# Three of eleven pairs of down-projection tiles as seven block products, in an encoder trunk on one core

## The chip, the cores and the metric

The kernel runs on one core of a Trainium2 chip. A core has the engines PE (TensorE: matmuls and transposes), DVE (VectorE), ACT (ScalarE), POOL (GpSimd) and SP (SyncE, here only a DMA queue). Each engine takes its own instructions in the order of its queue and waits on semaphores for the others. The metric is the device time of one execution in microseconds (us); less is better.

## The reference

Four layers, post-norm. The mixer is chunked band attention in layers 0 and 3, a gated linear attention in layer 1, differential attention in layer 2. Behind each mixer stands a dense SwiGLU feed-forward. All is float32; 256 tokens, width 1024, hidden width 2816.

```python
def swiglu(x, w_gate_up, w_down):
    g, u = jnp.split(x @ w_gate_up, 2, axis=-1)
    return (jax.nn.silu(g) * u) @ w_down

for i in range(DEPTH):                      # DEPTH = 4
    y = mixer_i(h)
    h = layer_norm(DN_ALPHA * h + y, ln1_g[i], ln1_b[i])
    h = layer_norm(DN_ALPHA * h + swiglu(h, ffn_w_gate_up[i], ffn_w_down[i]), ln2_g[i], ln2_b[i])
```

## The kernel before

A float32 product is made from two reduced-precision halves of each operand (type fp32r): a high part, which is a cast, and a low part, which is the difference of the value and its cast. A block product of two 128-row operands is three matmuls: high by high, low by high, high by low. Two functions issue them. `run_rows` has the tokens as the stationary side and 512 output columns, so one product is three matmuls of 128x512 (L176 to L178). `run_cols` has 128 weight columns as the stationary side and the 256 tokens as the moving one; there a product is one matmul of 512 columns (both parts of the tokens) and one of 256 (L197, L198).

**Weights.** `w_tiles` takes two k-tiles (256 rows) by 512 columns at a time: SP issues one load of 512 KB into a ring of 6 raw tiles (L110), ACT casts 128x1024 to the high part (L111), DVE subtracts to get the low part (L112), into rings of 8 tiles each.

**Activations.** `split_T` transposes 128x128 blocks on PE (L225) and `put` splits the result: a cast on ACT (L212), a subtraction on DVE (L213).

**Order.** The program is written in one order and a scheduler sets each engine's queue from it. Work that belongs behind a product (transposes, gates, norms) is put off with `defer` by a count of products (the D_ numbers); `tick` counts them.

**Feed-forward.** `ffn` (L844) computes hidden blocks of 256 columns. The first two blocks go through `run_rows` and `row_done` (silu on ACT at L856, product on DVE at L858, then `split_T`); the other nine go through `run_cols` and `col_done` (copy L869, additions L870, silu L872). All hidden values are kept as high and low parts, in 22 k-tiles. The down projection is one call of `run_rows`: 2 column halves x 22 k-tiles x 2 token blocks = 88 products, 264 matmuls in a layer.

**Norm.** `Norm.part` adds the residual (L277) and takes statistics (L288) as each half of the columns comes; `finish` aggregates (L301), has POOL compute the reciprocal root (`rstd_of`, L246 and L250), and scales (L308, L320). `late_load` brings gains and biases: POOL copies one column of a tile that stands for the right time (L123) and then issues the load (L124).

**Gated linear attention.** `gla` (L608) first sets up constants on POOL: a tile `cst` with a triangle of ones and the norm's gain (memset L614, L617 to L619, load L628), `g1t` for the first gate's weights (memset L638), `g2` for the second gate's weights and bias (memset L647, loads L648 to L650). Then `gate1` (L668), `gate2` (L688) and `gate3` (L701, L706) follow one another for each block of 128 tokens, among the products of the stage. The constants come from a pool of tiles (`k2`) that all stages share, eight deep.

**Start.** 16 transposes of the identity (L905) into an otherwise idle bank.

Of the kernel before, what the change touches and what calls it, by code (L numbers as in the profile page):

```python
# [25 lines left out]
RAWB = 6  # L26
WB = 8
WARM = 16
# [4 lines left out]
D_NORM, D_HIDDEN = 8, 4  # L33
# [3 lines left out]
def trunk_kernel(  # L37
# [30 lines left out]
    wp = ctx.enter_context(tc.tile_pool(name="wp", bufs=1))  # L68
    act = ctx.enter_context(tc.tile_pool(name="act", bufs=1))
# [7 lines left out]

    def slab(shape, dtype=F32):
        return act.tile(shape, dtype, tag="slab", bufs=4, name=nm("slab"))

    def k3(shape, dtype=F32):
        return act.tile(shape, dtype, tag="k3", bufs=5, name=nm("k3"))

    def k2(shape, dtype=F32):
        return act.tile(shape, dtype, tag="k2", bufs=8, name=nm("k2"))

    def k1(shape, dtype=F32):
        return act.tile(shape, dtype, tag="k1", bufs=6, name=nm("k1"))
# [13 lines left out]
    def w_tiles(chunk, s, fine=False):  # L102


        raw = wp.tile([P, 2, 512], F32, tag="raw", bufs=RAWB, name=nm("raw"))
        wh = wp.tile([P, 2, 512], F32R, tag="wh", bufs=WB, name=nm("wh"))
        wl = wp.tile([P, 2, 512], F32R, tag="wl", bufs=WB, name=nm("wl"))
# [10 lines left out]
        return [(wh[:, k, :], wl[:, k, :]) for k in range(2)]  # L118

# [22 lines left out]
    def run_rows(chunks, lag=LAG, order=None, fine=0):  # L142
# [16 lines left out]
        for t, c, kt in order:  # L159
# [9 lines left out]
            b = banks[c, t]  # L169
            first = count[c, t] == 0  # L170
# [67 lines left out]

    def kt_of(op):
        return lambda kt: op[:, kt, :]  # L240
# [14 lines left out]
    class Norm:  # L255
        def __init__(self, h, g_ap, b_ap, out_ap=None):
# [4 lines left out]
            self.g = act.tile([P, D], F32, tag="lng", bufs=1, name=nm("lng"))  # L261
            self.b = act.tile([P, D], F32, tag="lnb", bufs=1, name=nm("lnb"))
            self.loads = [
                (self.g, g_ap.partition_broadcast(P)),
                (self.b, b_ap.partition_broadcast(P)),
            ]

        def load(self, seen):

            if self.loads:  # L270
                late_load(*self.loads.pop(0), seen)

        def part(self, n):
            def done(t, y):
                z = self.h[t]
                cs = slice(n * 512, (n + 1) * 512)
                nc.vector.scalar_tensor_tensor(  # L277
                    out=z[:, cs],
                    in0=z[:, cs],
                    scalar=ALPHA,  # L280
                    in1=y,
                    op0=ALU.mult,
# [15 lines left out]
        def finish(self, t, st):  # L298
# [5 lines left out]
            if not last and self.xT is None:  # L304
                self.xT = operand()
# [712 lines left out]
```

## Time and profile before

| What | Value |
|---|---|
| Runs | 1207.79, 1210.9, 1211.17 us; median 1210.9 us |
| Profiled execution | 1210.89 us, of which the profiled span is 1209.2 us |
| PE busy | 1192.0 us, 99% of the span |
| DVE busy | 828.9 us, 69% |
| ACT busy | 664.4 us, 55% |
| POOL busy | 97.9 us, 8% |
| Chain of work that ended last | PE 94%, DVE 2% |

Busy time of PE is the time in which a matmul is under way; matmuls are pipelined, so the spacing of their starts is shorter than the length shown for one. In a group or a timeline row `out<-in` are the program's names for the tiles, and the line number is that of the kernel before. The granted clock of PE is 0.99 or more of full speed in nearly all of the span.

### The profile page before, as it was taken

To read this page: it belongs to the slowest core of one execution; us is meant where nothing else is said; L and a number is where in the kernel's file an instruction comes from. 1 tells how busy PE (TensorE), PEld (TensorE's weight loads), DVE (VectorE), ACT (ScalarE), POOL (GpSimd) and SP (SyncE) were. 2 spreads that over 40 slices of the span, in tenths; PEclk is the share of its full clock that TensorE was granted. 3 is DMA by queue.
4 is the path that set the end of the run, shared out by engine and by line. 5 is a ranking of instruction groups with operands and counts; after the bars stand their busy time and mean duration, and the time that the engine had idled before them with its cause. 6 is when DMAs were issued, how large, how long until landed. Compare 5 with 4: busy or idle time off the path is not lost.

```text
span 1209.2 us, 17119 instructions
## 1 busy us (share of the span) xinstructions
PE 1192.0 (99%) x6240; PEld 994.6 (82%) x6240; DVE 828.9 (69%) x1418; ACT 664.4 (55%) x1169; POOL 97.9 (8%) x188
## 2 busy tenths in 40 slices
PE   7999999999999999999999999999999999999997
PEld 6888888888787888888887778888888888888885
DVE  6688866755656766774757787667476988676644
ACT  6566565644664355663446656656345775565531
POOL 1130000000001100000012110000011200000000
PEclk9999999999999999999999999999999999999999
DMA  9654656556474456555664355665566644655641
GB/s 358 207 191 139 207 179 224 193 175 192 140 244 122 152 182 241 197 183 184 191 222 149 118 169 188 219 209 187 176 193 220 191 138 151 204 205 184 206 142 35
DMA packets 62772, 223.88 MB, mean 185 GB/s; under 512 B 7264, under 2 KB 7776, under 8 KB 62688
## 3 DMA queue, kind: packets, MB, share of 16 engines
q1 hardware_dynamic: 57600, 206.60, 51.9%
q0 software_dynamic: 4512, 15.14, 3.5%
q10 hardware_dynamic: 576, 1.05, 0.3%
q8 instruction: 49, 0.80, 0.3%
q14 instruction: 35, 0.29, 0.1%
HBM read 221.71 MB, written 1.05 MB: 184 GB/s over the span
## 4 chain that ended last, share of the span: by engine, by line
PE 94%; DVE 2%; ACT 1%; DMA 1%; POOL 1%; issue 0%; POOLq 0%; DVEq 0%; ACTq 0%
PE mm L197 28%; PE mm L176 15%; PE mm L177 15%; PE mm L178 15%; PE mm L198 15%; PE tp L225 2%; PE tp L423 2%; ACT k L446 1%; PE tp L492 1%; DVE k L431 1%; DMA k<-in_c_bias_dram 1%; PE tp L513 0%; PE tp L515 0%; PE tp L514 0%; PE tp L755 0%
## 5 line engine op out<-in xcount | busy, mean ns | idle before, releaser
L112 DVE TENSOR_TENSOR wl<-raw,wh 128x1024 fp32r<-128x1024 f32 (+1 forms) x394 | 476.1, 1213 | 173.8 <-ACT wh L111 170.3
L197 PE MATMUL mm<-slab,wh 128*128 128x512 f32 x1568 | 553.8, 396 | 0.0
L111 ACT CAST wh<-raw 128x1024 fp32r<-128x1024 f32 (+1 forms) x394 | 407.1, 1047 | 199.6 <-PE mm L177 186.7
L198 PE MATMUL mm<-slab,wl 128*128 128x256 f32 x1568 | 441.0, 281 | 0.0
L197 PEld LDWEIGHTS mm<-slab,wh 128*128 128x128 f32 x1568 | 294.1, 188 | 69.7 <-issue 4.6
L176 PE MATMUL mm<-wh,slab 128*128 128x512 f32 x784 | 309.9, 396 | 6.1 <-ACT wh L111 6.1
L177 PE MATMUL mm<-wh,slab 128*128 128x512 f32 x784 | 307.4, 392 | 0.0
L178 PE MATMUL mm<-wl,slab 128*128 128x512 f32 x784 | 306.5, 391 | 0.0
L198 PEld LDWEIGHTS mm<-slab,wl 128*128 128x128 f32 x1568 | 296.5, 189 | 0.7 <-issue 0.3
L176 PEld LDWEIGHTS mm<-wh,slab 128*128 128x128 f32 x784 | 147.3, 188 | 38.8 <-ACT wh L111 6.1
L177 PEld LDWEIGHTS mm<-wh,slab 128*128 128x128 f32 x784 | 147.5, 188 | 31.1 <-issue 1.5
L178 PEld LDWEIGHTS mm<-wl,slab 128*128 128x128 f32 x784 | 147.3, 188 | 30.4 <-DVE wl L112 0.3
L870 DVE TENSOR_TENSOR k<-mm,k 128x256 f32<-128x256 f32 x144 | 60.5, 420 | 79.4 <-ACT k L869 79.4
L869 ACT COPY k<-mm 128x256 f32<-128x256 f32 x144 | 53.6, 372 | 67.4 <-PE mm L198 67.1
L872 ACT ACTIVATE k<-k 128x256 f32<-128x256 f32 x72 | 29.8, 414 | 46.7 <-DVE k L870 46.7
L246 POOL TENSOR_SCALAR sm<-mv 128x1 f32<-128x1 f32 x16 | 14.0, 874 | 499.3 <-DVE mv L301 499.3
L212 ACT CAST slab<-k 128x256 fp32r<-128x256 f32 (+1 forms) x76 | 31.8, 418 | 38.8 <-DVE k L876 37.5
L213 DVE TENSOR_TENSOR slab<-k,slab 128x256 fp32r<-128x256 f32 (+1 forms) x76 | 33.0, 434 | 22.8 <-ACT slab L212 22.8
L446 ACT ACTIVATE k<-k,nmx 128x128 f32<-128x128 f32 x96 | 42.5, 444 | 8.4 <-DVE nmx L442 8.3
L212 ACT CAST slab<-tp 128x512 fp32r<-128x512 f32 (+1 forms) x56 | 27.1, 495 | 31.9 <-PE tp L225 29.3
L213 DVE TENSOR_TENSOR slab<-tp,slab 128x512 fp32r<-128x512 f32 (+1 forms) x56 | 30.6, 569 | 8.6 <-ACT slab L212 8.6
L431 DVE CUSTOM_DVE_ANT_0 k<-tp,k 128x128 f32<-128x128 f32 x96 | 28.5, 352 | 10.2 <-PE tp L423 9.0
(135 smaller groups left out, 675.5 us busy)
## 6 DMA issues: line engine op xcount, KB each, us to landing
raw<-in_w_gu_dram SPq DMA_DIRECT2D x176, 512.0 KB, 4.4
raw<-in_w_down_dram SPq DMA_DIRECT2D x88, 512.0 KB, 4.2
raw<-in_a_qkv_dram SPq DMA_DIRECT2D x46, 512.0 KB, 4.7
raw<-in_b_in_dram SPq DMA_DIRECT2D x24, 512.0 KB, 3.6
raw<-in_c_qkv_dram SPq DMA_DIRECT2D x24, 512.0 KB, 3.7
raw<-in_a_o_dram SPq DMA_DIRECT2D x16, 512.0 KB, 4.1
k<-in_a_bias_dram POOLq DMA_DIRECT2D x16, 256.0 KB, 4.4
lng<-in_ln_g_dram POOLq DMA_DIRECT2D x8, 512.0 KB, 5.6
```

Of the source, the lines that this page charges most:

```text
L111: nc.scalar.copy(out=wh[:, k, :], in_=raw[:, k, :])
L112: nc.vector.tensor_tensor(out=wl[:, k, :], in0=raw[:, k, :], in1=wh[:, k, :].bitcast(F32), op=ALU.subtract,)
L176: nc.tensor.matmul(b, xh, wh, start=first, stop=False)
L177: nc.tensor.matmul(b, xl, wh, start=False, stop=False)
L178: nc.tensor.matmul(b, xh, wl, start=False, stop=last)
L197: nc.tensor.matmul(b, wh[:, cs], xk, start=kt == 0, stop=False)
L198: nc.tensor.matmul(b[:, :256], wl[:, cs], xk[:, :256], start=False, stop=kt == NKT - 1)
L212: nc.scalar.copy(out=h, in_=val)
L213: nc.vector.tensor_tensor(out=dst[:, ks, slice(256 + cs.start, 256 + cs.stop)], in0=val, in1=h.bitcast(F32), op=ALU.subtract,)
L446: nc.scalar.activation(pr[:, m, SL[t]], pr[:, m, SL[t]], AF.Exp, bias=nmx[:, t, m : m + 1], accum_out=sm[:, t, m : m + 1],)
L869: nc.scalar.copy(out=lo, in_=b[:, 256:])
L870: nc.vector.tensor_tensor(out=lo, in0=b[:, :256], in1=lo, op=ALU.add)
```

## The change

**Down projection.** The weights are laid out by pairs of k-tiles: `w_down[layer, c]` is 128x2048, the four blocks (two k-tiles by two halves of 512 columns) of pair c, loaded in 1 MB pieces. For pairs 0, 3 and 6 of the 11 (`SEVEN`) the 2x2 product of blocks (two token blocks by two k-tiles, times two k-tiles by two column halves) is made from seven block products where it was eight, by the Winograd form: the blocks of hidden values are combined with four additions (`combine`, on POOL), the blocks of weights with four (three DVE instructions, `load`), the seven products go into banks that `FORMS` and `where` name, and `gather` adds them into the residual at the last such pair. The other eight pairs keep eight products. The last three pairs finish token block 0 first, then block 1. A product's three matmuls come in another order (high by low first).

**Memory.** The weight rings are counted in bytes (24 KB raw, 64 KB split, as deep as before for ordinary pairs). `k2`, `k3` and `slab` come from a pool that is opened for each stage (`in_stage`) and reuses the memory of the stage before tile by tile. The next stage's input has a tile of its own (`xT`). Gains and biases of a norm are loaded as four 128x512 tiles.

**Start.** 24 transposes, written into the first bank that the products use.

```diff
-D_NORM, D_HIDDEN = 8, 4
+D_NORM, D_HIDDEN, D_COMBO = 8, 4, 5
+WARM = 24
+SEVEN = (0, 3, 6)
...
+    def in_stage(fn, *args, **kw):
+        with tc.tile_pool(name=nm("stage"), bufs=1, reuse_waits="tile") as pool:
...
     def k2(shape, dtype=F32):
-        return act.tile(shape, dtype, tag="k2", bufs=8, name=nm("k2"))
+        return st(shape, dtype, "k2", 12)
...
+    def halves(w, n):
+        wh = split_ring.tile([P, n, 512], F32R, name=nm("wh"))
+        wl = split_ring.tile([P, n, 512], F32R, name=nm("wl"))
+        nc.scalar.copy(out=wh, in_=w)
+        nc.vector.tensor_tensor(out=wl, in0=w, in1=wh.bitcast(F32), op=ALU.subtract)
...
+            for _ in range(warm):
+                nc.tensor.transpose(b[:, :P], ident, ident)
+            warm = 0
...
+        def combine(c):
+            f = hidden.pop(c)
+            a11, a12, a22, s1, s2, s3, s4, a21 = (f[:, i, :] for i in range(8))
+            nc.gpsimd.tensor_tensor(out=s1, in0=a21, in1=a22, op=ALU.add)
+            nc.gpsimd.tensor_tensor(out=s2, in0=s1, in1=a11, op=ALU.subtract)
+            nc.gpsimd.tensor_tensor(out=s3, in0=a11, in1=a21, op=ALU.subtract)
+            nc.gpsimd.tensor_tensor(out=s4, in0=a12, in1=s2, op=ALU.subtract)
+            defer(D_COMBO, lambda: split(c, f))
+
+        def split(c, f):
+            x = seven[c] = st([P, 2, 7, P], F32R, "seven", len(SEVEN))
+            nc.scalar.copy(out=x[:, 0], in_=f[:, 0:7, :])
+            nc.vector.tensor_tensor(
+                out=x[:, 1], in0=f[:, 0:7, :], in1=x[:, 0].bitcast(F32), op=ALU.subtract
+            )
...
-                defer(D_HIDDEN, lambda: split_T(hd, hid[0], t, 2 * c, 2))
+                defer(D_HIDDEN, lambda: turn_hidden(c, t, hd))
...
+            h11 = halves(raw[:, 0:1], 1)
+            diff(tt[:, 0:2, :], raw[:, 1:3, :], raw[:, 0:2, :])
+            diff(t2, tt[:, 1, :], b11, ALU.add)
+            ht = halves(tt, 3)
+            diff(t4, b21, t2)
+            parts[c] = h11 + halves(raw[:, 1:4], 3) + ht
...
+            nc.tensor.matmul(o, xh, wl, start=start, stop=False)
+            nc.tensor.matmul(o, xh, wh, start=False, stop=False)
+            nc.tensor.matmul(o, xl, wh, start=False, stop=stop)
...
+        FORMS = {
+            1: (0, 0), 6: (4, 6), 5: (3, 4), 7: (5, 5), 2: (1, 3), 3: (6, 2), 4: (2, 1),
+        }
...
+        tail = range(n_pairs - 3, n_pairs)
+        load(0)
+        for c in range(n_pairs - 3):
+            load(c + 1)
+            if c in SEVEN:
+                seven_products(c)
+                continue
...
-    idle = bank()
-    for _ in range(WARM):
-        nc.tensor.transpose(idle[:, :P], ident, ident)
```

On ACT, in layer 0 where the feed-forward goes from row products to column products, the queue before (casts of weights wh, silu of the last row block L856, casts of transposed hidden values into the operand):

```order
L212 CAST slab_1381<-tp_1498 128x2x128 [waits PE_49]
L111 CAST wh_1654<-raw_1653 128x1024 [waits DVE_49,DMAHW4_49,PE_49,Activation_49]
L111 CAST wh_1660<-raw_1659 128x1024 [waits DVE_49,DMAHW5_49,PE_49,Activation_49]
L856 ACTIVATE k_338_1518<-mm_1488 128x256 [waits PE_49,Activation_49]
L212 CAST slab_1381<-tp_1559 128x2x128 [waits PE_49]
```

and after (hid: the hidden blocks of a seven pair; seven: their operand with the sums; L932 is the silu):

```order
L959 COPY hid_1441<-tp_1518 128x128 [waits PE_49]
L960 COPY hid_1441<-tp_1518 128x128
L130 CAST wh_1679<-raw_1678 128x1024 [waits DMAHW4_49,DVE_49,PE_49]
L924 CAST seven_1546<-hid_1441 128x896 [waits Activation_49,Pool_49]
L932 ACTIVATE k_341_1542<-mm_1508 128x256 [waits DVE_49,PE_49]
L130 CAST wh_1685<-raw_1684 128x1024 [waits DMAHW5_49,DVE_49]
L244 CAST plain_1348<-tp_1586 128x2x128 [waits PE_49]
```

The cast L924, which waits for POOL's sums, now stands ahead of the silu, and one weight cast has moved behind it.

On PE at the same place, before (L197 and L198 are column products, L225 the transposes of the last row block's hidden values):

```order
L198 MATMUL mm_1546<-slab_1258,wl_1536 128x256
L197 MATMUL mm_1546<-slab_1258,wh_1541 128x512 [waits Activation_49]
L198 MATMUL mm_1546<-slab_1258,wl_1542 128x256
L197 MATMUL mm_1546<-slab_1258,wh_1541 128x512
L225 MATMUL tp_1559<-ident,k_339_1520 128x128 [waits DVE_49,PE_49]
```

and after (L229 and L230 are the column products, L943 the transposes):

```order
L229 MATMUL mm_1573<-xT_1276,wh_1562 128x512
L230 MATMUL mm_1573<-xT_1276,wl_1563 128x256
L943 MATMUL tp_1586<-ident,k_342_1544 128x128 [waits DVE_49]
L943 MATMUL tp_1586<-ident,k_342_1544 128x128
L229 MATMUL mm_1573<-xT_1276,wh_1568 128x512 [waits Activation_49]
```

The transposes of the last row block stand three column matmuls earlier (12 such matmuls are ahead of them, where 15 were).

On POOL at the start of the gated layer, before (L246 and L250 are the reciprocal root of the norm, L123 and L124 bring the next gain):

```order
L676 MEMSET k_658_3159 1x128 [waits DVE_49,Activation_49]
L246 TENSOR_SCALAR sm_597_2918<-mv_2916 128x1 [waits DVE_49,Pool_49]
L250 TENSOR_TENSOR sm_598_2920<-sm_597_2918,powt 128x1 [waits Pool_49]
L246 TENSOR_SCALAR sm_605_2978<-mv_2976 128x1 [waits DVE_49]
L250 TENSOR_TENSOR sm_606_2980<-sm_605_2978,powt 128x1 [waits Pool_49]
L123 COPY lng_2986<-slab_3009 128x1 [waits DMASW0_49,DVE_49]
L124 DMA lng_2986<-in_ln_g_dram 128x1024 [waits DMASW3_49,Pool_49]
```

and after (L282 and L286 are the reciprocal root; k_625, k_627 and k_628 are `cst`, `g1t` and `g2`):

```order
L282 TENSOR_SCALAR sm_620_3027<-mv_3025 128x1 [waits DVE_49]
L286 TENSOR_TENSOR sm_621_3029<-sm_620_3027,powt 128x1 [waits Pool_49]
L660 MEMSET k_625_3039 128x512 [waits PE_49,Activation_49]
L684 MEMSET k_627_3049 128x512
L663 MEMSET k_625_3039 64x64 [waits Pool_49]
...
L674 DMA k_625_3039<-in_b_g_norm_dram 128x256 [waits DMASW3_49]
L665 AFFINE_SELECT k_625_3039<-k_625_3039 128x128 [waits Pool_49]
L693 MEMSET k_628_3053 128x512
L694 DMA k_628_3053<-in_b_w_g_dram 16x512 [waits Pool_49]
L695 DMA k_628_3053<-in_b_w_g_dram 16x512
L696 DMA k_628_3053<-in_b_b_g_dram 1x16x32 [waits DMASW6_49]
L150 COPY k_708_3397<-slab_3060 128x1 [waits DVE_49]
```

The set-up of the constants has moved from the middle of layer 0's attention, ahead of that layer's two norms, to a place behind the second block's reciprocal root at the end of the layer.

On PE there, before (L688 is the second gate, L225 the transposes of the second token block):

```order
L688 MATMUL tp_3057<-k_614_3002,k_625_3032 128x512 [waits DMASW5_49,DMASW4_49,DMASW6_49,DVE_49,Pool_49]
L176 MATMUL mm_3016<-wh_3049,slab_2922 128x512
...
L178 MATMUL mm_3016<-wl_3070,slab_2922 128x512
L225 MATMUL tp_3080<-ident,h_75 128x128 [waits DVE_49,PE_49]
L225 MATMUL tp_3080<-ident,h_75 128x128 x3
L176 MATMUL mm_3093<-wh_3088,slab_2922 128x512
```

and after (L734 is the second gate, L257 the transposes, L747 the third gate):

```order
L734 MATMUL tp_3108<-k_628_3053,k_639_3083 128x512 [waits DMASW5_49,DMASW4_49,DMASW6_49,DVE_49,Pool_49]
L257 MATMUL tp_3141<-ident,h_77 128x128 x4
L257 MATMUL tp_3151<-ident,h_77 128x128 x4
L208 MATMUL mm_3167<-wh_3062,xT_2965 128x512 [waits Activation_49]
...
L208 MATMUL mm_3167<-wh_3100,xT_2965 128x512 [waits Activation_49]
L209 MATMUL mm_3167<-wh_3100,xT_2965 128x512 [waits DVE_49]
L210 MATMUL mm_3167<-wl_3101,xT_2965 128x512
L747 MATMUL tp_3174<-k_648_3110,k_625_3039 128x512 [waits DVE_49,PE_49]
```

The transposes of the second block stood nine matmuls behind the second gate and now stand directly behind it; between them and the third gate are 16 matmuls of products.

At the start of PE's queue the transposes of the identity (L200, 24 of them) stand ahead of the first product's matmuls; before, the 16 of L905 stood behind three matmuls.

## Rows read from the trace of the kernel before

**Rows 1.** The page's list of engines: busy us, share of the span, instructions.

```profile
PE 1192.0 (99%) x6240; PEld 994.6 (82%) x6240; DVE 828.9 (69%) x1418; ACT 664.4 (55%) x1169; POOL 97.9 (8%) x188
```

**Rows 2.** What PE waited for: us in total, times, longest.

```profile
PE mm L176 <- ACT wh L111: 6.1, 1, 6.1
```

**Rows 3.** Timeline of PE in a down projection: start, length, line, operation.

```profile
573.99 0.39 PE L176 MATMUL mm<-wh,slab 128*128 128x512 f32 x1
...
576.94 0.39 PE L177 MATMUL mm<-wh,slab 128*128 128x512 f32 x1
```

**Rows 4.** Busy time by engine (PE, PEld, DVE, ACT, POOL) in a down projection.

```profile
544.00:574.00 30.00, 30.00 (x135) 24.82 (x134) 14.04 (x18) 10.78 (x12) 0.00 (x0) 1.00 0.56 187
```

**Rows 5.** Timeline of PE at the start: identity transposes, fifth k-tile's last matmul.

```profile
7.52 3.10 PE L905 MATMUL tp<-ident 128*128 128x128 f32 x16
...
14.35 0.39 PE L178 MATMUL mm<-wl,slab 128*128 128x512 f32 x1
```

**Rows 6.** Timeline of DVE at the start: subtractions of weights, two shapes.

```profile
10.55 0.69 DVE L112 TENSOR_TENSOR wl<-raw,wh 128x512 fp32r<-128x512 f32 x1 [0.66 <-ACT wh L111]
...
12.52 1.22 DVE L112 TENSOR_TENSOR wl<-raw,wh 128x1024 fp32r<-128x1024 f32 x1 [0.67 <-ACT wh L111]
```

**Rows 7.** Timeline of DVE in layer 0's feed-forward, row to column products.

```profile
142.81 2.42 DVE L112 TENSOR_TENSOR wl<-raw,wh 128x1024 fp32r<-128x1024 f32 x2
...
145.68 2.58 DVE L112 TENSOR_TENSOR wl<-raw,wh 128x1024 fp32r<-128x1024 f32 x2
148.18 0.41 DVE L858 TENSOR_TENSOR k<-k,mm 128x256 f32<-128x256 f32 x1
```

**Rows 8.** Timeline of ACT at the same place.

```profile
143.87 0.36 ACT L212 CAST slab<-tp 128x256 fp32r<-128x256 f32 x1
144.59 1.06 ACT L111 CAST wh<-raw 128x1024 fp32r<-128x1024 f32 x1 [0.36 <-ACT slab L212]
...
146.90 0.38 ACT L856 ACTIVATE k<-mm 128x256 f32<-128x256 f32 x1
```

**Rows 9.** Timeline of POOL in layer 0's attention: the same copy twice.

```profile
46.58 1.11 POOL L123 COPY k<-slab 128x1 f32<-128x1 f32 x1 [3.02 <-DVE slab L397]
...
54.65 0.19 POOL L123 COPY h<-slab 128x1 f32<-128x1 f32 x1 [0.83 <-DVE slab L397]
```

**Rows 10.** Timeline of DVE at the first of them.

```profile
46.43 1.22 DVE L112 TENSOR_TENSOR wl<-raw,wh 128x1024 fp32r<-128x1024 f32 x1
```

**Rows 11.** Timeline of PE in the feed-forward: transposes of the last row block.

```profile
148.74 0.41 PE L225 MATMUL tp<-ident,k 128*128 128x128 f32 x2
```

**Rows 12.** Timeline of POOL: first, one middle and last instruction of the constants.

```profile
81.05 0.53 POOL L614 MEMSET k<- 128x512 f32 x1
...
82.99 0.29 POOL L619 TENSOR_SCALAR_AFFINE_SELECT k<-k 128x128 f32<-128x128 f32 x1
...
86.65 0.56 POOL L650 DMA_DIRECT2D k<-in_b_b_g_dram  x1
```

**Rows 13.** Timeline of POOL at the end of layer 0: the reciprocal root.

```profile
310.41 1.05 POOL L246 TENSOR_SCALAR sm<-mv 128x1 f32<-128x1 f32 x1 [7.74 <-DVE mv L301]
311.55 0.94 POOL L250 TENSOR_TENSOR sm<-sm,powt 128x1 f32<-128x1 f32 x1
```

**Rows 14.** Timeline of DVE there: addition and statistics, later the second gate's end.

```profile
307.61 0.68 DVE L277 SCALAR_TENSOR_TENSOR h<-h,mm 128x512 f32<-128x512 f32 x1
...
309.34 0.68 DVE L288 BATCH_NORM_STATS2 bnst<-h 128x6 f32<-128x512 f32 x1
...
317.57 0.69 DVE L694 SCALAR_TENSOR_TENSOR k<-tp,k 128x512 f32<-128x512 f32 x1 [1.25 <-ACT k L693]
```

**Rows 15.** DMA issues, 80 to 95 us: engine, KB, median us to landing.

```profile
k<-in_b_b_g_dram POOLq DMA_DIRECT2D x1, 2.0 KB, 3.6
```

**Rows 16.** Timeline of PE at the gated layer's start: first gate, second gate.

```profile
308.44 1.10 PE L668 MATMUL tp<-slab,k 128*128 128x256 f32 x8
...
311.44 1.02 PE L688 MATMUL tp<-k,k 65*128 65x512 f32 x2
```

More of the change, by code (lines that the diff above doesn't have):

```diff
@@ L603, in attention @@
             run_cols(wqkv[g], src, qk_done(g))
-            norm.load(qk_all[:, g, 2, 0:1])
+            for _ in range(2):
+                norm.load(qk_all[:, g, 2, 0:1])
         out_proj(OT, w_o, norm)
@@ L886, in ffn @@
             run_cols(w[c], src, col_done(c))
-            if c % 2 == 0:
-                norm.load(hid_kt(2 * c + 1)[:, 0:1].bitcast(F32))
-        run_rows(
-            [
-                (w_down[layer, n], range(NHT), hid_kt, norm.part(n))
-                for n in range(2)
-            ]
-        )
+            if c >= 7:
+                k = place_of(c)
+                norm.load(
+                    plain[:, k, 0:1].bitcast(F32), lambda sh: st(sh, F32, "gb", 4)
+                )
+        parts = {}
@@ new lines, in into, with seven_products @@
+        def into(key, x, w, stop):
+            if key not in bk:
+                bk[key] = bank("mm" if len(bk) < 4 else "tp")
+            product(bk[key], x, w, key not in begun, stop)
+            begun.add(key)
+        def seven_products(c):
+            for i, (a, b) in FORMS.items():
+                x = seven[c]
+                into(
+                    where.get(i, i),
+                    (x[:, 0, a, :], x[:, 1, a, :]),
+                    parts[c][b],
+                    c == SEVEN[-1] and i not in where,
+                )
+                if c == SEVEN[-1]:
+                    gather(i)
+            del parts[c], seven[c]
@@ new lines, in ffn, with step @@
+        place = {(0, 0): 0, (0, 1): 1, (1, 0): 3, (1, 1): 2}
+        def step(t, n, c, k, last=False):
+            x = plain[:, place_of(c) + k, :]
+            into(
+                (t, n),
+                (x[:, t * P : (t + 1) * P], x[:, 2 * P + t * P : 2 * P + (t + 1) * P]),
+                parts[c][place[k, n]],
+                last,
+            )
+            if last:
+                norm.part(n)(t, bk[t, n])
+        tail = range(n_pairs - 3, n_pairs)
[5 more added lines that the diff above has]
+                continue
+            for t in range(2):
+                for k in range(2):
+                    for n in range(2):
+                        step(t, n, c, k)
@@ L897, in trunk_kernel @@
+        for c in tail[1:]:
+            load(c)
+        end = (n_pairs - 1, 1)
+        for n in range(2):
+            for c in tail:
+                for k in range(2):
+                    step(0, n, c, k, (c, k) == end)
+        for c in tail:
+            for n in range(2):
+                for k in range(2):
+                    step(1, n, c, k, (c, k) == end)
     h = [act.tile([P, D], F32, tag=f"h{t}", bufs=1, name=nm("h")) for t in range(2)]
-    xT = operand()
+    xT = input_operand()
@@ L920, in trunk_kernel @@
             norm1.loads = [
[L921 removed]
+                (h[t], None, x[0, t * P : (t + 1) * P, :]) for t in range(2)
             ] + norm1.loads
[L923 removed]
+            first = dict(src=first_src, lag=2, fine=4, warm=WARM)
         else:
```

196 lines of the change are left out of this document (143 added, 53 removed).

## The prediction

> **What bounds the kernel now.** I read the page's engine list first: the matmul engine is busy 1192.0 us of a 1209.2 us span [rows 1]. Then the list of what PE waited for: its largest entry is 6.1 us, once, for the first weights [rows 2]. That leaves 1209.2 - 1192.0 - 6.1 = 11.1 us for the tail behind the last matmul and for all else: between its first matmul and its last PE is dense. The change does not touch the tail. Hence only two things can move the time: how many matmuls are issued, and whether some new wait opens a hole in PE. An engine other than PE can cost something only where PE reaches an instruction whose operand is late.
>
> The price of a matmul comes from the timeline in a down projection: from 573.99 to 576.94 there are 13 starts, one after another, 2.95 / 13 = 0.227 us each (the 0.39 shown is the pipelined length, not the spacing) [rows 3]. A block product is three of them, 0.68 us. In 30 us of a down projection DVE works 14.04 us, ACT 10.78 and POOL nothing [rows 4].
>
> **Part 1, fewer products: -8.2 us.** Three of eleven pairs take seven products where eight stood, in four layers: 12 products x 3 matmuls x 0.227 = 8.2 us. Every one of them lay in a dense stretch, so this is a gain on the path. It is the only large term with a minus.
>
> **Part 2, the warm-up: -0.6 us (0 to -0.6).** Before, the 16 transposes run at 7.52, behind the first product, and PE is dense afterwards [rows 5]. After, the transposes run while the first weights are still on their way. What this gives back is limited by the weights: the low part of the fifth k-tile is ready at 12.52 + 1.22 = 13.74 [rows 6] and is used at 14.35 [rows 5], so PE can come at most 0.61 us earlier before it waits for DVE there. I take all of it.
>
> **Part 3, differences of weights on DVE: +0.8 us (0 to +8).** A seven pair costs DVE the differences, one of 1024 columns and two of 512, and the splits of 3584 columns: at 1.22 for 1024 and 0.69 for 512 [rows 6], 2.6 + (0.69 + 1.76 + 1.76, the two splits of 1536 columns scaled from 0.69 and 1.22) = 6.8 us. Its products last 7 x 0.68 = 4.8 us on PE. A plain pair needs 2 x 1.22 = 2.4 of DVE against 5.4 of PE. Over a seven pair and two plain ones DVE has 11.7 us to do in 15.7 us of PE. DVE is thus short by 2.0 us in the seven pair and long by 6.0 in the two behind it, and the rings (same bytes as before) let it run ahead by about two pairs. The first pair of a stage is a seven pair, and DVE comes to it from the gate and up projections with its ring full; I take 0.2 us per layer. If that lead were gone, 2.0 per layer, or 8, would be the price.
>
> **Part 4, the sums of hidden blocks on POOL: +7.4 us (0 to +12.4).** This is the term that decides. For pair 0 the four sums are made where row products end and column products begin. In the order of ACT, the silu of the last row block stands behind the cast of the seven operand, which waits for the sums; that silu feeds a product on DVE and two transposes, and the transposes stand in PE's queue, now three matmuls earlier than before. So PE waits for POOL there. I place the chain on the times of layer 0:
> - The two copies of the hidden block take the place of the ACT cast at 143.87 and end about 144.4 [rows 8]. DVE runs weight differences from 142.81 to 145.23 [rows 7].
> - POOL and DVE do not work side by side: a one-column copy on POOL takes 0.19 us when DVE is free, but 1.11 when it begins under a 1.22 us weight subtraction that starts at 46.43, and it ends just behind that one [rows 9, 10]. So the first sum ends near 145.23 + 0.4 = 145.63.
> - The next cast on ACT (144.59 + 1.06) [rows 8] lets DVE start the following subtraction at 145.68 [rows 7]; it holds POOL to 146.90. The other three sums end at 146.90 + 3 x 0.4 = 148.10.
> - The cast of 896 columns, 0.94 by scaling the 1.06 for 1024 [rows 8], ends at 149.04; silu 0.38 [rows 8] at 149.42; the product 0.41 [rows 7] at 149.84; PE can transpose near 149.99.
> - PE comes to the transposes at 148.74 [rows 11] less three matmuls (0.58) = 148.16. The hole is 1.8 us, and 4 layers make 7.4.
>
> A sum of two 128x128 operands on POOL is not in the trace. The nearest rows are the one-input 128x128 selection at 0.29 [rows 12], and the power over a 128x1 pair of operands at 0.94 [rows 13]. I take 0.4, close to the selection because size and engine match. At 0.25 to 0.3 each and with no lock the sums end by 146.0 and the hole is gone; with each sum held for about 1.05, as a locked copy is, the hole is 3.1 us and the term 12.4. Pairs 3 and 6 have whole column blocks of slack and cost nothing.
>
> [...]
>
> **Part 5, constants of the gated layer: +5.0 us (0 to +8).** Before, POOL prepared them at 81.05 to 86.65, over 200 us ahead of use [rows 12]. Now they live in the stage's own memory, which is the FFN's; POOL's first memset waits for the last matmul that reads the FFN's plain operand, and it is queued behind the second block's reciprocal root. Let E be the end of layer 0's down projection (307.5; the first addition of the norm follows at 307.61 [rows 14]).
> - The norm of the second block: one addition 0.68, two statistics of 0.68 [rows 14], one weight subtraction of 1.22 between [rows 6], and two POOL steps, 1.05 and 0.94 [rows 13]; with the short aggregate these make 5.3, so near E + 5.5.
> - The set-up: 81.05 to 87.21 without the 1.9 us that belong to other work there (a bias load, another memset and idle time) is 4.2 us [rows 12], so the last load is issued by E + 9.7 and lands 3.6 us after it was begun [rows 15]: about E + 13.2.
> - PE does 16 products (10.9) and the first gate's eight matmuls (1.1 [rows 16]) and is at the second gate at E + 12.0. Hole: 1.2 us. The first gate itself needs its constant cast and subtracted in two pieces: 0.3.
> - What stands behind the second gate in PE's queue: the second block's transposes, whose operand comes through an ACT cast and a subtraction (0.4), then the third gate. From the end of the second gate to the end of its elementwise chain the trace has 311.44 + 1.02 to 317.57 + 0.69 = 5.8 us [rows 14, 16]; PE has 16 matmuls and eight transposes between, 3.6 + 1.2. Hole: 1.0.
> - The second block's gates follow at six matmuls where the trace has more; that distance is not in it. Bounds are 0 and the first block's 1.2 + 0.4 + 1.0 = 2.6; I take 2.1, as its ACT has two weight casts in front.
> The sum is 5.0. Behind the set-up on POOL stand only the gains of the next norm, needed much later.
>
> **The sum.** -8.2 - 0.6 + 0.8 + 7.4 + 5.0 = +4.4. The profiled execution took 1210.89, as long as the median of the three runs, 1210.9. Forecast: 1215.3 us. A difference under 0.3% (3.6 us: 1207.3 to 1214.5) can't be told from no change.
>
> **Rivals.**
> - A, the sums slip in. If they end by 148.16 - 0.15 - 0.41 - 0.38 - 0.94 = 146.28, PE finds its transposes ready; that is decided by whether all four fit in 144.4 to 146.28, under 0.47 each with no lock. The time is 1215.3 - 7.4 = 1207.9 and not slower. For it: 0.29 for the selection; against: DVE is in a subtraction for nearly all of that stretch. 0.18.
> - B, the gated layer hides its constants (loads land by E + 12.0, and the gates' chains overlap): 1215.3 - 5.0 = 1210.3. For it: the hole at the second gate is small against a chain of 13 us; against: the later holes have the order's short distances. 0.10.
> - C, both: 1202.9, faster; the products' saving comes out nearly whole. 0.06.
> - D, dear sums (each held by DVE): 1215.3 + 5.0 = 1220.3; or DVE without its lead in the first pair, at 2.0 per layer, 1222.5. Together 0.14.
>
> **How the numbers follow.** The forecast has 0.52, and spreads over 1212 to 1218.5; two thirds of it lie above 1214.5. A straddles 1207.3 evenly. Faster: 0.06 + 0.09 = 0.15. Same: 0.17 + 0.09 + 0.10 = 0.36. Slower: 0.35 + 0.14 = 0.49. The range leaves out C, some of A's low half and the dearest half of D: 1207 to 1222. The forecast's own range is 1212 to 1218.5.
>
> **What would show it.** Right: PE's list of waits has the down transposes' line (hidden product on DVE) four times, at 1 to 3 us each, with the chain passing POOL's sums; near E + 12 a wait for the second gate's loads or memset, and one for the third gate; DVE's share in a down projection goes up and PE stays dense there. POOL's sums read 0.3 to 0.5 free and over 1 under a subtraction. Wrong: sums below 0.3 throughout and no wait at the transposes (A or C); waits on the low weights in the first pair of a down projection (D); or PE's busy time not down by about 8 us, in which case the first term is wrong.

## The result, and the profile after

The changed kernel takes 1226.9 us (median of four runs, 1226.8 to 1227.6) against 1211.0 for the kernel before: a ratio of 1.013, 95% interval 1.0113 to 1.0147. The direction was forecast, the size was not: +15.8 us, where +4.4 was forecast and the range ended at 1222.

The page's list of engines of the kernel after (busy us, share of the span, instructions), which answers [rows 1]:

```profile
PE 1199.9 (98%) x6212; PEld 990.0 (81%) x6212; DVE 899.6 (73%) x1490; ACT 680.6 (56%) x1185; POOL 147.1 (12%) x268
```

PE issues fewer matmuls and is busy 7.9 us longer. The prediction named this as the sign that its first term is wrong. What PE waited for in the kernel after (us in total, times, longest), which answers [rows 2]:

```profile
PE tp L943 <- DVE k L934: 6.1, 4, 1.6
PE tp L624 <- DVE k L611: 1.5, 2, 0.8
PE tp L734 <- DMA k<-in_b_b_g_dram: 1.5, 1, 1.5
PE tp L747 <- DVE k L740: 1.5, 2, 1.0
PE mm L200 <- POOL ident masks.py:199: 1.4, 1, 1.4
PE mm L208 <- ACT wh L130: 1.3, 1, 1.3
PE mm L210 <- DVE wl L131: 0.5, 1, 0.5
```

The forecast holes are there: four at the down transposes (L943), one at the second gate's loads (L734), one large one at the third gate (L747). They are not where the other 11 us went. Most of the rest is in the spacing of matmuls that wait for nothing. Timeline of PE in layer 0's down projection of the kernel after, two starts that are 30 matmuls apart, which answers [rows 3]:

```profile
269.67 0.40 PE L1027 MATMUL tp<-wl,plain 128*128 128x512 f32 x1
...
276.71 0.39 PE L1027 MATMUL tp<-wl,plain 128*128 128x512 f32 x1
```

(276.71 - 269.67) / 30 = 0.235 us, not 0.227. With 1020 such matmuls (255 in a layer) that is about 7.9 us by these starts. The column products of the gate and up projections show the same kind of thing. Timeline of PE, starts of the 512-column matmul that are 28 pairs apart (a pair is one of 512 and one of 256 columns); the kernel before in layer 0 and in layer 3:

```profile
199.73 0.39 PE L197 MATMUL mm<-slab,wh 128*128 128x512 f32 x1
...
209.44 0.39 PE L197 MATMUL mm<-slab,wh 128*128 128x512 f32 x1
...
1099.73 0.40 PE L197 MATMUL mm<-slab,wh 128*128 128x512 f32 x1
...
1109.64 0.40 PE L197 MATMUL mm<-slab,wh 128*128 128x512 f32 x1
```

and the kernel after in layer 0:

```profile
199.80 0.40 PE L229 MATMUL mm<-xT,wh 128*128 128x512 f32 x1
...
209.69 0.40 PE L229 MATMUL mm<-xT,wh 128*128 128x512 f32 x1
```

A pair takes 9.71 / 28 = 0.347 us in layer 0 before, 9.91 / 28 = 0.354 in layer 3 before, and 9.89 / 28 = 0.353 after, there in all four layers. The kernel before thus had both spacings for the same code; its layers 1 and 2 run like layer 0. Each layer has some 288 pairs, and 288 x 0.0067 = 1.9 us; three layers went from the fast spacing to the slow one, 5.8 us.

The tail grew too. The last matmul of the kernel before and that of the kernel after:

```profile
1200.37 0.39 PE L178 MATMUL mm<-wl,slab 128*128 128x512 f32 x1
...
1214.51 0.39 PE L1029 MATMUL tp<-wh,plain 128*128 128x512 f32 x1
```

Behind them the span has 1209.2 - 1200.4 = 8.8 us before and 1224.9 - 1214.5 = 10.4 after. VectorE ends its work 5.5 us behind the last matmul in both; the 1.6 us lie behind that, in the end of the program, and why isn't known.

### The profile page after: what moved, and what is told of

It is laid out like the page before. It is cut to its first block, busy times and chain, and to the rows that moved or that the text cites. A ratio compares the mean times of both kernels' runs of the same rounds, so it can differ in the third digit from the quotient of the medians.

```text
span 1224.9 us, 17125 instructions
## 1 busy us (share of the span) xinstructions
PE 1199.9 (98%) x6212; PEld 990.0 (81%) x6212; DVE 899.6 (73%) x1490; ACT 680.6 (56%) x1185; POOL 147.1 (12%) x268
## 4 chain that ended last, share of the span: by engine, by line
PE 89%; POOL 3%; DVE 2%; DMA 2%; ACT 2%; issue 2%; POOLq 0%; DVEq 0%; ACTq 0%
PE mm L229 28%; PE mm L230 14%; PE mm L208 7%; PE mm L209 7%; PE mm L210 7%; PE tp L1027 5%; PE tp L1029 5%; PE tp L1028 5%; PE tp L468 2%; PE tp L257 1%; PE mm L1027 1%; PE mm L1028 1%; PE mm L1029 1%; PE tp L537 1%; DMA k<-in_c_bias_dram 1%
## 5 line engine op out<-in xcount | busy, mean ns | idle before, releaser
L229 PE MATMUL mm<-xT,wh 128*128 128x512 f32 x1568 | 559.3, 400 | 0.0
L230 PE MATMUL mm<-xT,wl 128*128 128x256 f32 x1568 | 441.4, 281 | 0.0
L229 PEld LDWEIGHTS mm<-xT,wh 128*128 128x128 f32 x1568 | 294.8, 188 | 74.3 <-issue 4.6
L230 PEld LDWEIGHTS mm<-xT,wl 128*128 128x128 f32 x1568 | 296.5, 189 | 0.7 <-issue 0.3
L208 PE MATMUL mm<-wh,xT 128*128 128x512 f32 x304 | 120.1, 398 | 1.6 <-ACT wh L130 1.3
L210 PE MATMUL mm<-wl,xT 128*128 128x512 f32 x304 | 119.4, 393 | 0.6 <-DVE wl L131 0.5
L209 PE MATMUL mm<-wh,xT 128*128 128x512 f32 x304 | 119.5, 394 | 0.0
L1027 PE MATMUL tp<-wl,plain 128*128 128x512 f32 x256 | 102.0, 398 | 0.0
L1028 PE MATMUL tp<-wh,plain 128*128 128x512 f32 x256 | 101.5, 396 | 0.0
L1029 PE MATMUL tp<-wh,plain 128*128 128x512 f32 x256 | 101.4, 396 | 0.0
L208 PEld LDWEIGHTS mm<-wh,xT 128*128 128x128 f32 x304 | 56.9, 188 | 15.9 <-ACT wh L130 2.3
L209 PEld LDWEIGHTS mm<-wh,xT 128*128 128x128 f32 x304 | 57.1, 188 | 13.4 <-issue 1.2
L1029 PEld LDWEIGHTS tp<-wh,plain 128*128 128x128 f32 x256 | 48.2, 188 | 11.8
L282 POOL TENSOR_SCALAR sm<-mv 128x1 f32<-128x1 f32 x16 | 11.9, 746 | 380.6 <-DVE mv L346 380.6
L1028 PEld LDWEIGHTS tp<-wh,plain 128*128 128x128 f32 x256 | 48.2, 188 | 11.5
```

Source lines behind the costliest of these rows:

```text
L208: nc.tensor.matmul(b, xh, wh, start=first, stop=False)
L209: nc.tensor.matmul(b, xl, wh, start=False, stop=False)
L210: nc.tensor.matmul(b, xh, wl, start=False, stop=last)
L229: nc.tensor.matmul(b, wh[:, cs], xk, start=kt == 0, stop=False)
L230: nc.tensor.matmul(b[:, :256], wl[:, cs], xk[:, :256], start=False, stop=kt == NKT - 1)
L1027: nc.tensor.matmul(o, xh, wl, start=start, stop=False)
```

## Experiments

All times are medians on the chip; the kernel before was run beside each, and its median went from 1209.1 to 1211.0. So a difference between the medians of two experiments is uncertain by up to some 2 us; the spacings, read from the traces, are not.

**shift_stage: the place of the operands.** Two tiles are said here to start at the same place when their addresses leave the same rest on division by 2048 bytes. In the compiled program of the kernel before, the operands (slabs) start at the same place as the weight rings, at 672. In the changed one the stage's memory begins at 1792, while rings and xT (the operand that holds a stage's input) are still at 672. Nothing in the diff says so; it follows from the sizes of the small tiles that lie ahead. The experiment puts 32 unused bytes ahead of the stage's memory, which makes 1824. START and ORDER are the names of two theories.

```diff
     def in_stage(fn, *args, **kw):
+        if "shift" not in moved:
+            moved["shift"] = act.tile([P, 8], F32, tag="shift", bufs=1, name="shift")
+            nc.gpsimd.memset(moved["shift"], 0.0)
```

> The changed kernel with one unused tile of 32 bytes ahead of the stage's memory: every operand that stages keep (plain, seven, the attention outputs) now starts at 32 modulo 64 bytes, like the weight rings, where it started at 0. Nothing else changes. Theory START (a matmul is slower when its stationary operand and its moving one start at different places within 64 bytes): the matmuls of the down projection go from 0.234 us apart back to 0.227, those of the out projections too; about 1020 x 0.0075 = 7.6 us and 384 x 0.0075 = 2.9 us, so near 1216.5. Theory ORDER (the new order of a product's three matmuls, or the banks used, makes them slower): spacing stays 0.234 and the time 1226.9.

1218.4 us, ratio 1.0076 (1.0061 to 1.0091). Near the time that START gave, but not by its way. Timeline of PE in the down projection, 30 matmuls apart:

```profile
269.71 0.39 PE L1032 MATMUL tp<-wh,plain 128*128 128x512 f32 x1
...
276.68 0.40 PE L1032 MATMUL tp<-wh,plain 128*128 128x512 f32 x1
```

6.97 / 30 = 0.232: less than 0.235, far from 0.227, some 2 us. The larger part came from the column pairs, which ran at 9.70 / 28 = 0.346 in all four feed-forwards here (199.92 to 209.62 in layer 0), though their operands had not moved. Two questions follow: how exact must the place be, and what switches the column pairs?

**order_before: the order of a product's matmuls.**

```diff
-            nc.tensor.matmul(o, xh, wl, start=start, stop=False)
-            nc.tensor.matmul(o, xh, wh, start=False, stop=False)
-            nc.tensor.matmul(o, xl, wh, start=False, stop=stop)
+            nc.tensor.matmul(o, xh, wh, start=start, stop=False)
+            nc.tensor.matmul(o, xl, wh, start=False, stop=False)
+            nc.tensor.matmul(o, xh, wl, start=False, stop=stop)
```

> The changed kernel with the three matmuls of a down product in the order of the kernel before (high by high, low by high, high by low). Theory ORDER: spacing in the down projection 0.227, about 7.6 us less, 1219. Theory START: spacing stays 0.234 and the time within 1.5 us of 1226.9.

1226.5 us, spacing unchanged (269.78 to 276.81, 30 matmuls: 0.234). The order is out. So are the banks that `FORMS` and `where` name: the next run keeps them.

**align_stage: the exact place.** As shift_stage with 928 bytes (`[P, 232]`).

> The changed kernel with 928 unused bytes ahead of the stage's memory, so that plain and the attention outputs start at the same place within 2048 bytes (672) as the weight rings, as all operands of the kernel before did; 32 bytes brought the down matmuls only from 0.234 to 0.232 us apart. Theory START in its finer form (the place within more than 64 bytes counts): down and out projections at 0.227, some 5 to 7 us less than with 32 bytes: 1212 if the column pairs stay at 0.347, 1219 if they fall back to 0.353. Rival (only the place within 64 bytes counts, and the rest of the slower spacing is due to something else): 0.232 and 1218.4.

1219.6 us, ratio 1.007 (1.0055 to 1.0085). Timeline of PE in the down projection, 30 matmuls apart:

```profile
269.78 0.39 PE L1031 MATMUL tp<-wl,plain 128*128 128x512 f32 x1
...
276.58 0.39 PE L1031 MATMUL tp<-wl,plain 128*128 128x512 f32 x1
```

6.80 / 30 = 0.227, the spacing of [rows 3]. The column pairs stayed at 0.353 here, so the 7.3 us are row products alone; in the traces the four down projections are 7.1 us shorter. START in its finer form fits: at 672, like the rings, they have 0.227, and at 1824, the same place within 64 bytes, they had 0.232 (shift_stage). Whether the span that counts is 2048 bytes or a smaller one, no run tells.

**minus32: which way round.** As align_stage with 896 bytes (`[P, 224]`), so 32 bytes below the rings' place.

> The changed kernel with the stage's memory 32 bytes below the rings' place within 2048 bytes (640, not 672). Theory DISTANCE (any difference of place between stationary and moving operand costs): down matmuls at 0.232 to 0.234 us, 1225 to 1227. Theory SIGN (it costs only where the stationary operand starts behind the moving one; in the column pairs with xT 32 bytes off it starts ahead, and they were fast): 0.227, near 1219.6 as in align_stage.

1220.0 us. The down matmuls are 30 apart in 7.00 us:

```profile
269.79 0.40 PE L1032 MATMUL tp<-wh,plain 128*128 128x512 f32 x1
...
276.79 0.40 PE L1032 MATMUL tp<-wh,plain 128*128 128x512 f32 x1
```

0.233, so DISTANCE holds and SIGN falls. The time is not the 1225 to 1227 expected, because the column pairs were at 0.347 in all four feed-forwards again. A total alone would have pointed to the wrong theory.

**before_shift: the same done to the kernel before.** 32 unused bytes ahead of its slabs; nothing else.

```diff
     h = [act.tile([P, D], F32, tag=f"h{t}", bufs=1, name=nm("h")) for t in range(2)]
+    shift = act.tile([P, 8], F32, tag="shift", bufs=1, name="shift")
+    nc.gpsimd.memset(shift, 0.0)
```

> The kernel before with 32 unused bytes ahead of its operands (slabs), which then start at 0 modulo 64 while the weight rings start at 32. Theory START: 2352 row matmuls go from 0.227 to 0.234 apart, up to 17 us, and the column pairs may stay slow in all layers, up to 6 us more: 1220 to 1234. Theory ORDER: no change, 1211.

1218.6 us, ratio 1.0076 (1.0061 to 1.0091): 9.4 us for 32 bytes, with not one instruction changed on PE. That is a little below the expected range. Its down matmuls:

```profile
269.74 0.40 PE L176 MATMUL mm<-wh,slab 128*128 128x512 f32 x1
...
276.74 0.40 PE L176 MATMUL mm<-wh,slab 128*128 128x512 f32 x1
```

0.233. But the column pairs were fast in all four layers (199.84 to 209.55 for 28 pairs: 0.347), layer 3 too. So 32 bytes off took longer where the activations are the stationary operand (0.233 for 0.227), and had the faster of the two spacings where they are the moving one (0.347 in all layers, for 0.354 in layer 3 before).

**shift_input: xT off as well.** The changed kernel with the line of before_shift. It moves xT 32 bytes off the rings, and the stage's memory behind it to 1824, as in shift_stage.

> The changed kernel with the same 32 bytes ahead of the input operand xT too, so that xT starts at 0 modulo 64, and the stage's operands at 32 like the weight rings. Theory START: down projection and out projections at 0.227, but all products that read xT get the slower spacing: row products on xT 0.234, column pairs at 0.353 or more. Time between 1217 and 1226. Theory ORDER: no change, 1226.9.

1221.5 us, ratio 1.0097. The row products on xT came out as expected, at 0.233 (617.82 to 624.82 for 30). The down matmuls did not: 0.233 (269.83 to 276.81), as at 1824 before. The column pairs too came out against the expectation, fast in all four layers (199.69 to 209.40: 0.347).

**nudge: the state of the column pairs.** One unused transpose on PE ahead of them.

```diff
                 nc.tensor.transpose(b[:, ks], hd[:, ks], ident)
+            if c == 1 and t == 1:
+                nc.tensor.transpose(b[:, 256:384], hd[:, :P], ident)
             if c not in SEVEN:
```

> The changed kernel with one more 128x128 transpose on PE behind the down transposes of the last row block in each layer, its result unused. Theory MODE (the column pairs behind it run in one of two states, 0.347 or 0.353 us, which is set by the moment at which PE starts on them and then stays): the state may change in some layers; each layer that changes gives 288 x 0.0067 = 1.9 us back, four of them 7.7: down to 1219.5. Rival (the spacing is set by addresses or by what other engines do): stays at 0.353 everywhere, 1227.

1223.7 us, ratio 1.0102 (1.0083 to 1.0122). In the profiled execution one layer of four changed. Timeline of PE, 28 pairs in layer 1 (still slow) and in layer 2 (now fast):

```profile
459.82 0.40 PE L229 MATMUL mm<-xT,wh 128*128 128x512 f32 x1
...
469.71 0.40 PE L229 MATMUL mm<-xT,wh 128*128 128x512 f32 x1
...
757.93 0.40 PE L229 MATMUL mm<-xT,wh 128*128 128x512 f32 x1
...
767.64 0.40 PE L229 MATMUL mm<-xT,wh 128*128 128x512 f32 x1
```

9.89 against 9.71 us, same addresses, same code. One layer is worth 1.9 us; the four executions range from 1221.0 to 1225.9.

**sums_dve: the sums on VectorE.** `nc.gpsimd` becomes `nc.vector` in the four lines of `combine`.

> The changed kernel with the four sums of hidden blocks on VectorE instead of POOL. Theory POOL (the holes before the down transposes come from POOL's sums held up by VectorE): the wait of 6.1 us in four pieces goes, or shrinks to under 1 us; 1220 to 1221. If it is not the sums but the cast of 896 columns or the order of ACT, 3 us or more of the wait stay. A theory of the column pairs' spacing rides along: if the slow spacing of 0.353 us per pair is set by how PE comes out of the hole, it may go back to 0.347 in the four feed-forwards, 7 us more: 1213.

1219.8 us, ratio 1.0069 (1.0052 to 1.0086): 7.1 less, and no wait at the down transposes is left. What POOL did in the changed kernel (timeline of POOL in layer 0):

```profile
143.18 1.34 POOL L918 TENSOR_TENSOR hid<-hid 128x128 f32<-128x128 f32 x1 [15.45 <-ACT hid L959]
144.48 0.46 POOL L916 TENSOR_TENSOR hid<-hid 128x128 f32<-128x128 f32 x1
145.01 1.33 POOL L917 TENSOR_TENSOR hid<-hid 128x128 f32<-128x128 f32 x1
146.42 0.46 POOL L919 TENSOR_TENSOR hid<-hid 128x128 f32<-128x128 f32 x1
```

and the end of its chain on PE:

```profile
148.65 0.44 PE L943 MATMUL tp<-ident,k 128*128 128x128 f32 x2 [1.51 <-DVE k L934]
```

Here a sum takes 0.46 us, and 1.33 or 1.34 where it starts while DVE is in a weight subtraction (141.75 to 144.19, 144.54 to 146.02). In sums_dve one sum is 0.28 us on DVE. Two more things changed there: the scheduler put the silu ahead of the cast on ACT, and the transposes stand behind 16 column matmuls on PE, where they stood behind 12. Timelines of DVE and PE in sums_dve, the product that the transposes wait for and the transposes:

```profile
147.18 0.41 DVE L934 TENSOR_TENSOR k<-k,mm 128x256 f32<-128x256 f32 x1
...
147.66 0.42 PE L943 MATMUL tp<-ident,k 128*128 128x128 f32 x2
```

The product starts at 147.18 here and at 148.17 in the changed kernel, 1.0 us later, where the hole was 1.5 us: by this the earlier product closes about two thirds of it, and the four matmuls that now stand ahead fill the rest. So the 7.1 us are for all three changes; none was tried alone. The column pairs stayed slow.

**gla_const: constants in their own memory,** set up ahead of layer 0's feed-forward in program order; POOL's queue then has them at the start.

```diff
-        return st(shape, dtype, "k2", 12)
+        return st(shape, dtype, "k2", 9)
...
+    def cg(dtype):
+        return act.tile([P, 512], dtype, tag="cg", bufs=3, name=nm("cg"))
...
+        if i == 0:
+            gla_setup()
```

> The changed kernel with the gated layer's constants in memory of their own, set up at the program's start (the stage's k2 tiles go from 12 to 9 to make room). Theory: the waits for the second gate's loads (1.5 us), for the third gate (1.5) and the small ones around them go, 3 to 5 us less: 1222 to 1224. Rival (the order of PE alone, transposes directly behind the second gate, makes these waits): under 1.5 us less.

1222.8 us, ratio 1.0096 (1.0081 to 1.0111), 4.1 less. The wait for the loads is gone, that for the third gate is 0.2. But two other things changed. First, the order on PE: the transposes of the second block, which stood directly behind the second gate, stand 12 matmuls behind it here (L745 is the second gate, L257 the transposes; timeline of PE):

```profile
314.54 1.10 PE L745 MATMUL tp<-cg,k 65*128 65x512 f32 x2
...
318.23 0.60 PE L257 MATMUL tp<-ident,h 128*128 128x128 f32 x4
```

So the run doesn't part the constants from the order. The wait for the loads was one for the constants, by its own row; whether the third gate waited for the order or for the late second gate stays open. Second, the column pairs of layer 2 ran fast in the profiled execution. Timeline of PE, 28 pairs:

```profile
755.76 0.39 PE L229 MATMUL mm<-xT,wh 128*128 128x512 f32 x1
...
765.47 0.39 PE L229 MATMUL mm<-xT,wh 128*128 128x512 f32 x1
```

9.71 us, 1.9 less for the layer, with nothing changed in its code. By the traces, PE's stretch from layer 0's last down matmul to layer 1's first column pair of the feed-forward is 137.8 us in the kernel after and 133.9 here, 3.9 less, and the start is 0.9 longer.

**all_three: the repairs together.** align_stage, sums_dve and gla_const.

> The changed kernel with all three repairs: stage memory at the same place within 2048 bytes as the weight rings (measured alone 1219.6), sums on VectorE (alone 1219.8), the gated layer's constants in memory of their own (alone 1222.8). If the repairs add up: 1226.9 - 7.3 - 7.1 - 4.1 = 1208.4; each feed-forward whose column pairs go to 0.347 us gives 1.9 less, down to 1200.7. Rival (repairs overlap, as a hole that is filled shows the next late thing): 1210 or more.

1208.8 us, ratio 0.9987 (0.9977 to 0.9998): the repairs add up to within 0.4 us. That is closer than it should be, and in part luck: gla_const had one layer's column pairs fast in its profiled execution, and here all of them are slow.

**eight: without the seven products.** all_three with `SEVEN = ()`.

> As all_three, but no pair takes the seven-product form (SEVEN is empty): all eleven pairs with eight products. Shows what the seven products give by themselves when the rest is repaired. Theory (12 products x 0.68 us = 8.2 us, all on the path): 8.2 us slower than all_three, less what the differences and sums cost there (0 to 3 us): 5 to 8 us. A change in the column pairs' state, 1.9 us per layer, has to be taken out first. Rival (VectorE is the bound in the down projection, and the saving is lost to it): under 3 us.

1215.0 us (1213.0 to 1218.2), 6.1 more than all_three by the medians; the profiled spans are 1216.5 and 1208.2, 8.3 apart, and each is the longest execution of its kernel. The column pairs are slow in both. In the traces the four down projections, from first to last matmul, are 7.8 us longer together without the seven products. So they give nearly what the first term said with the spacing of 0.227 that align_stage, one of the repairs, had alone.

**all_three_input: xT 32 bytes off as well.**

> As all_three, with the input operand xT 32 bytes off the weight rings. Theory (column pairs that read xT at another place than the rings always run at 0.347 us, as they did in shift_input and before_shift; row products on xT then take 0.233): column pairs 7.7 us less than if all are slow, some 900 row matmuls x 0.006 = 5.3 us more: 1206. Against all_three it is 2.4 us less if that one's pairs are all slow, and up to 5.3 more if they are all fast.

1205.0 us, ratio 0.9958 (0.9944 to 0.9972). 0.4% below the kernel before. Column pairs are at 0.346 in all layers (199.90 to 209.60). Four layers at 1.9 us would make 7.7 less than all_three, and the time is 3.8 less; by estimate the other 3.9 went to the row products on xT, which were at 0.233 in shift_input.

**three_nudge1, 2, 3: another moment of the start.** all_three with one, two and three unused transposes, as in nudge.

> As all_three, with one more 128x128 transpose on PE in each layer, behind the down transposes of the last row block (result unused). Addresses are those of all_three. Theory MODE (where xT and the rings start at the same place, the column pairs have two states, 0.347 and 0.353 us, and the moment at which PE starts on them picks one, which then stays): some layers change to 0.347, each 1.9 us less than all_three (1208.8): 1201 to 1209 by the number that change. Rival (the state hangs on addresses alone): all layers at 0.353 as in all_three, 1209.

> As three_nudge1 with two more transposes in each layer. Theory MODE: another set of layers may change; 1201 to 1209. Rival: 0.353 everywhere, 1209.

> As three_nudge1 with three more transposes in each layer. Theory MODE: another set of layers may change; 1201 to 1209. Rival: 0.353 everywhere, 1209.

1209.7, 1207.2 and 1203.7 us. In the profiled executions no layer of four ran fast with one transpose, layers 0 and 3 with two, all four with three. Timeline of PE in layer 0 of three_nudge3, 28 pairs:

```profile
199.75 0.40 PE L233 MATMUL mm<-xT,wh 128*128 128x512 f32 x1
...
209.45 0.40 PE L233 MATMUL mm<-xT,wh 128*128 128x512 f32 x1
```

9.70 us, 0.346 a pair; in three_nudge1 it is 199.60 to 209.49, 0.353. The first half of MODE is shown: where both operands start at the same place, there are two states at the same addresses, 0.346 to 0.347 us a pair and 0.353, and in the feed-forwards of the kernel before each lasts for the whole stage: in all stretches of 20 us it is 0.347 from 160 to 240 us (layer 0) and 0.353 from 1040 to 1140 (layer 3). The rival, addresses alone, falls. That the moment of the start picks the state is not shown: a transpose also changes what stands ahead. The number of transposes alone doesn't decide: one changed a layer in nudge and none in three_nudge1, and layer 2 changed in gla_const without any. With two transposes the executions spread from 1204.2 to 1212.4, as if the pick were not always the same. three_nudge3, ratio 0.9959 (0.9945 to 0.9974), is the fastest version run, and level with all_three_input.

## Why the prediction was wrong

**The step that failed is "Hence only two things can move the time: how many matmuls are issued, and whether some new wait opens a hole in PE".** There is a third, the price of the matmuls that stay, and the prediction put its change at nothing without a reason. The term "12 products x 3 matmuls x 0.227" itself was nearly right: in eight the down projections are 7.8 us longer. But 0.227, read from a down projection of before, was carried to the 255 matmuls of a layer that remain. Their operand had moved to other memory, and they took 0.235: about 7.9 us by the count, 7.3 when align_stage put it back. Where the prediction speaks of the stage's memory, in part 5, it speaks of waits only. PE's busy time, up by 7.9 us, was named as the sign of a wrong first term; it was the sign of this.

**A second term was missing: the column pairs,** +5.8 us. The prediction took the gate and up projections as untouched. The trace of before held the warning, 0.354 in layer 3 beside 0.347 in layer 0, but only the down projection's spacing was read. Seen, it would have widened the range by up to 1.9 us a layer. Which layers would run slow couldn't be foreseen: edits that touch none of this code changed them, so this term is in part bad luck.

**Part 4 (sums on POOL, +7.4) was right in place and nearly in size.** The four holes are 6.1 us in the list of waits, and 7.1 went with sums_dve, whose other order had a part in it. The path was a little different: no third subtraction held the last sums; two of the four were held for 1.33 us each, and a free one took 0.46, not 0.4; 0.3 to 0.5 free and over 1 when held had been given as signs. (Four holes of 1.83 make 7.3, not 7.4.) On DVE, in sums_dve, a sum took 0.28.

**Part 5 (constants, +5.0) was right in its total:** PE's stretch from layer 0's last down matmul to the first column pair of layer 1's feed-forward grew from 132.9 to 137.8 us, by 4.9, and gla_const took 3.9 of that back. Timeline of PE in the kernel after, second and third gate:

```profile
322.94 1.10 PE L734 MATMUL tp<-k,k 65*128 65x512 f32 x2 [1.51 <-DMA k<-in_b_b_g_dram]
...
330.38 1.10 PE L747 MATMUL tp<-k,k 128*128 128x512 f32 x2 [0.97 <-DVE k L740]
```

The holes were put at 1.2 and 1.0. For the second block, put at 2.1, one wait of 0.5 at its third gate is all that the list has. With 0.3 for an operand that ACT casts (L208) the four waits make 3.3 us; the rest of the 4.9 stands in no wait of the list, so the total agrees better than its parts do.

**Part 2 (start, -0.6):** the fifth k-tile's last matmul comes at 13.55 after, at 14.35 before [rows 5]: -0.8, a little past the bound of 0.6, since DVE had that low part done at 13.50 and at 13.74 before; and, as forecast, PE waits there for DVE, 0.53 us:

```profile
13.55 0.50 PE L210 MATMUL mm<-wl,xT 128*128 128x512 f32 x1 [0.53 <-DVE wl L131]
```

**Part 3 (DVE, +0.8):** no wait of PE on the low weights of a down projection is in the list. None of the rivals came: A and C needed no holes, B none in the gated layer, D dear sums or a bound on DVE. The true rival, the same matmuls at another spacing, was not among them.

**The tail.** "The change does not touch the tail" was wrong by 1.6 us in the profiled execution, for a reason that stays open.

**The account,** by stretches of PE in the two profiled executions, whose spans are 15.7 us apart:
- The four down projections, from first to last matmul, are 0.9 us shorter together: -8.2 (products) + 7.3 (row spacing).
- The four stretches of column pairs in the feed-forwards are 12.0 longer: 6.1 (holes at the down transposes) + 5.8 (spacing) explain 11.9.
- What lies between layer 0's down projection and the column pairs of layer 1's feed-forward is 4.9 longer (constants, with the out projection's spacing).
- The start, up to the first column pair of layer 0's feed-forward, is 1.1 shorter, and the same stretches of layers 2 and 3 are 0.9 shorter together.
- The tail is 1.6 longer.

That makes -0.9 + 11.9 + 4.9 - 1.1 - 0.9 + 1.6 = +15.5, against 15.8 measured.

## What to carry to other kernels

Before a cost per instruction is carried over an edit of pools or tiles, compare where the operands of the busiest engine start, before and after: here one unused tile of 32 bytes was worth 9.4 us, on an engine whose waits come to 6.8 of 1216.6 us (before_shift). Read the spacing of starts in every stage and layer, not the busy share: two spacings for the same code in one trace, here 0.347 and 0.354 in the kernel before, can change with an edit elsewhere, as 0.353 became 0.347 in layer 2 of gla_const. And test a repair by the row that it should change, since two changes in spacing can cancel or imitate each other in the total. Compare the order of the engines too: a scheduler may answer a repair with another order, as in sums_dve and gla_const.

## What the runs showed of the hardware

- A matmul of 512 columns with activations as the stationary operand and weights as the moving one came every 0.227 us where both start at the same place within 2048 bytes (672; before, align_stage), and every 0.232 to 0.235 with the activations at 640, 704, 1792 and 1824 (minus32, before_shift, after, shift_stage). Why, no run tells.
- Pairs of column matmuls (weights stationary, activations moving) ran at 0.347 us in every feed-forward with the activations 32 bytes off the weights' place (before_shift, shift_input, all_three_input). With both at the same place they ran at 0.347 or 0.353 for a whole stage (before, after). Layers that had 0.353 ran at 0.346 to 0.347 with one to three extra transposes ahead of them (one in nudge, two in three_nudge2, four in three_nudge3; none in three_nudge1), and with edits elsewhere (layer 2 in gla_const, all layers in shift_stage and minus32). What picks the state, no run tells.
- Of the 48 sums of 128x128 on POOL, 16 started under a weight subtraction on DVE and took 1.32 to 1.38 us, and the other 32 took 0.45 to 0.46 (after); on DVE one took 0.28 (sums_dve).
